# Modulation matmuls placed behind the delta step's matmuls in the attention loop of a two-layer trunk

## The chip, the core and the metric

One core of a Trainium2 chip runs the whole program in one launch. The metric is device microseconds for one execution. TensorE (PE) multiplies, VectorE (DVE), ScalarE (ACT) and GpSimd (POOL) do the element work, SyncE (SP) issues transfers; GpSimd and ScalarE issue some too. Each engine runs its own list of instructions in the order in which it was written, and waits on semaphores for the others and for transfers.

## What is computed

Two layers of a diffusion trunk over 512 latent and 256 context tokens of width 1024. In each layer half of the width goes through grouped-query softmax attention, the other half through a gated delta rule, chunked by 64 tokens and run in both directions; both share an output projection. A mixture-of-experts follows (best group of 4, two of its 8 experts). Shifts, scales and gates of every norm come from the conditioning vectors by a weight of 1024 x 6144 per layer.

```python
# one chunk of the delta rule (per head and direction)
v_new = u_i - w_i @ state
o_i   = qd_i @ state + a_i @ v_new
state = state * exp(gl_i) + kd_i.T @ v_new
# attention of 8 heads over 2 key heads
p = softmax(q @ k.T * ATTN_SCALE);  a = p @ v
# output projection, and the modulation of all six parts
y = concat([a, rms_norm(o, dn_norm_w) * silu(gate)]) @ w_out
mod = silu(c) @ ada_w + ada_b      # shift, scale, gate of mixer and FFN
```

## The kernel before

The change lies in the attention loop of `layer` (L1628 to L1648), which runs once per layer. It mixes three generators by a pattern string: `d` takes the next part of a delta step, `f` fills with attention (scores `sc` L604, transposes `ptr` L626, values `pv` L645, transposed queries `qt` L589), and `a` takes one part of the modulation. There are 12 delta steps. One step issues on TensorE: `ks` (old state times keys, L898), `pz` (32 matmuls, L917), `su` (32, the state's update, L932), `po` (L948) and `pq` (L898). Its inputs `lk`, `lx`, `lq` are loaded on SP (L864, L865, L869) into two buffers each, and GpSimd multiplies `lx` by `lq` (L870) when they have landed. GpSimd also scales the old state (`se`, L905) and copies outputs (`o`, L965).

One modulation part (`ada_part`, L258) loads 1 MB of `ada_w` on GpSimd's queue into one of two buffers (`araw`, L231), issues 8 matmuls on TensorE (`aps`, L265, four column groups by two row blocks; the trace has 16 records of them) and adds the result to `ac` (L267 on ScalarE, L269 on VectorE). Four parts make one of the six thousand-column pieces; its sum is stored to `md` in DRAM. Layer 0's loop runs 24 parts, layer 1's 16.

The order of every engine is not the source's. A list scheduler takes the whole program, with its own estimate of durations, and puts out each engine's instructions when they seem ready; dependencies given by hand bind it. The `pin` helper, which chains instructions in source order, is switched off in this loop. So a single bound can move instructions far behind it.

Behind the loop comes the tail: the four quarters of `w_out` (`wr`, loaded on SP, L1062) are split into a high part on ScalarE (`woh`, L1069) and a low part on VectorE (`wol`, `wr`, `m1`, L1070). For each block of 128 tokens ScalarE converts the attention's rows (`al`, loaded L1040, converted L1041) and the transposed delta output (`ot`, L1045, L1047), the low parts come from GpSimd (L1042) and VectorE (L1048), TensorE makes two groups `po` of 24 matmuls (L239), VectorE multiplies by the gate (`ytm`, L1090) and GpSimd adds to the stream (`xs`, L1091). Norm and routing follow (L1055 to L1218). `g2`, `m3`, `s4` are the modulation rows read back from `md`: once for the context blocks, once more for the latent blocks (L1712, L1714). `sw` (L307) belongs to the table of the next layer.

Of the kernel before, what the change touches and what calls it, by code (L numbers as in the profile page):

```python
# [29 lines left out]
HD = 64  # L30
# [7 lines left out]
UNIT = 256  # L38
# [106 lines left out]
class Model:  # L145
    def __init__(self, ctx, tc, t):
        self.tc, self.nc, self.t = tc, tc.nc, t
        self.cp = ctx.enter_context(tc.tile_pool(name="const", bufs=1, side=L))
        self.pst = ctx.enter_context(ExitStack())
        self.psum(*PSA)  # L150
        self.dr = ctx.enter_context(tc.tile_pool(name="dr", bufs=1, space=DRAM))
        cst = self.cp.tile([P, CST.shape[1]], F32, name="cst")
        self.cst = cst
        self.nc.scalar.dma_start(cst[:, :CFIRST], t["cst"][:, :CFIRST])
        self.C = {k: cst[:, o:o + n] for k, (o, n) in CCOL.items()}
        self.ident = self.C["ident"]
        self.pins(False)
        self.seq = None
        self.mh = self.cp.tile([P, 32], F32, name="mh")
        self.nc.vector.memset(self.mh, -0.5)  # L160


    def pin(self, ins):

        if self.pinned:
            e = ins.ins.engine.name
            if self.last.get(e):
                self.tc.add_manual_dep(ins.ins, self.last[e], mybir.DependencyInfo(mybir.DependencyClass.NoSync, mybir.DependencyReason.DATA), reason="order")
            self.last[e] = ins.ins.name
        return ins  # L170
# [86 lines left out]
    def ada_part(self, i, ch, n, acc, cols, pool, bufs, q):  # L257

        nc = self.nc
        src = self.t["ada_w"][i].rearrange("(p k) n -> p k n", k=8)  # L260
        raw = self.wload(pool, src[:, 2 * n:2 * n + 2, ch * D:(ch + 1) * D], bufs, "araw", q=q)
        ps = self.psC("aps")
        for r in range(2):
            for g in range(4):
                self.pin(nc.tensor.matmul(ps[32 * g:32 * g + 32, :UNIT], self.sc[:, 2 * n + r, :], cols(raw[:, r, :], g), start=(r == 0), stop=(r == 1), tile_position=(0, 32 * g)))  # L265
        if n == 0:
            self.pin(nc.scalar.activation(acc, ps[:, :UNIT], AF.Copy))  # L267
        else:
            self.pin(nc.vector.tensor_tensor(acc, acc, ps[:, :UNIT], op=OP.add))  # L269
# [608 lines left out]
    def delta_step(self, s, S, kx, dT, sc, o, seen, need, pool):  # L878

        nc, pin = self.nc, self.pin  # L880
        ch, half, rows, tl, col = self.step_place(s)
        st = sc["st"][:, s]
        k, x = kx
        old = S[0]
        H = lambda a: a.rearrange("p (h e) -> p h e", e=HD)
        E = lambda a: a.rearrange("p (r e i) -> p r e i", e=2, i=HD)
        y, kn, xa, aa = H(k[:, 0]), H(k[:, 1]), H(x[:, 0]), H(x[:, 1])
        B4 = lambda a, e: a.rearrange("p (r e) -> p r e", e=2)[:, :, e, None].to_broadcast([P, 4, HD])

        def by_state(j, name):  # L890

            ps = [self.psC(name + str(e)) for e in range(2)]
            for pr in range(4):
                for a in range(2):
                    for e in range(2):
                        d = a ^ e
                        r = slice(64 * e, 64 * e + 64)
                        pin(nc.tensor.matmul(ps[e][rows[d], pr * HD:(pr + 1) * HD], dT[j][r, pr, col[d]:col[d] + 64], old[r, d, pr], start=True, stop=True, tile_position=(64 * e, half[d])))  # L898
            return [p[:, :256].rearrange("p (r i) -> p r i", r=4) for p in ps]

        if s > 0:
            ks = by_state(1, "ks")
            if s < 11:
                se = pool.tile([P, 2, 4, HD], F32, tag="se", bufs=1, name="se")
                getattr(nc, QUEUE["se"]).tensor_tensor(se, old, sc["el"][:, s, :, :, None].to_broadcast([P, 2, 4, HD]), op=OP.mult)  # L905
            yield
            t = pool.tile([P, 512], F32, tag="yt2", bufs=1, name="yt2")
            for e in range(2):
                pin(nc.vector.tensor_tensor(E(t)[:, :, e], ks[e], B4(st[:, 0], e), op=OP.mult))
            pin(nc.vector.tensor_tensor(k[:, 0], k[:, 0], t, op=OP.add))  # L910
        else:
            yield
        yield
        pz = self.psC("pz")
        for h in range(NH):
            for d in range(2):
                pin(nc.tensor.matmul(pz[rows[d], h * HD:(h + 1) * HD], xa[rows[d], h], y[rows[d], h], start=True, stop=True, tile_position=(half[d], half[d])))  # L917
        yield
        if s < 11:
            w = pool.tile([P, NH, HD], F32, tag="w", bufs=1, name="w")  # L920
            pin(nc.vector.tensor_tensor(w, H(pz), st[:, 2, :, None].to_broadcast([P, NH, HD]), op=OP.mult))
        if need:
            z = pool.tile([P, NH, HD], F32, tag="z", bufs=1, name="z")
            pin(nc.scalar.activation(z, H(pz), AF.Copy))
        yield
        if s < 11:
            su = [self.psC("su%d" % d) for d in range(2)]
            for pr in range(4):
                for a in range(2):
                    for d in range(2):  # L930
                        e = a ^ d
                        pin(nc.tensor.matmul(su[d][64 * e:64 * e + 64, pr * HD:(pr + 1) * HD], kn[rows[d], 2 * pr + e], w[rows[d], 2 * pr + e], start=True, stop=True, tile_position=(half[d], 64 * e)))  # L932
        yield
        if s < 11:
            new = pool.tile([P, 2, 4, HD], F32, tag="S", bufs=2, name="S")
            for d in range(2):
                u = su[d][:, :256].rearrange("p (r i) -> p r i", r=4)
                if s > 0:
                    pin(nc.vector.tensor_tensor(new[:, d], u, se[:, d], op=OP.add))
                else:  # L940
                    pin(nc.scalar.activation(new[:, d], u, AF.Copy))
            S[0] = new
        yield
        if need:
            po = self.psC("po")
            for h in range(NH):
                for d in range(2):
                    pin(nc.tensor.matmul(po[rows[d], h * HD:(h + 1) * HD], aa[rows[d], h], z[rows[d], h], start=True, stop=True, tile_position=(half[d], half[d])))  # L948
            if s > 0:
                pq = by_state(0, "pq")  # L950
        yield
        if need:
            t = pool.tile([P, 512], F32, tag="ot", bufs=2, name="ot")
            if s > 0:
                for e in range(2):
                    pin(nc.vector.tensor_tensor(E(t)[:, :, e], pq[e], B4(st[:, 1], e), op=OP.mult))
                pin(nc.vector.tensor_tensor(t, t, po, op=OP.add))
            else:
                pin(nc.scalar.activation(t, po, AF.Copy))
            for d in range(2):  # L960
                dst = o[rows[d], tl[d]]
                if ch[d] in seen:
                    nc.gpsimd.tensor_tensor(dst, dst, t[rows[d]], op=OP.add)
                else:
                    nc.gpsimd.tensor_copy(dst, t[rows[d]])  # L965
                    seen.add(ch[d])
        yield
# [555 lines left out]
    def layer(self, i, xsrc, rows, done, xstack, mod):  # L1523

        nc, tc, t = self.nc, self.tc, self.t
# [100 lines left out]
        with self.pool("at", B) as pool:  # L1626
# [9 lines left out]
            with self.pool("q2", A) as p2:  # L1636
                S, seen = [None], set()
                load = lambda s: s < 12 and self.step_load(s, vk, xad, qkd, need(D0[s] // 2), p2)
                kx = load(0)
                self.pins(False)  # L1640
                for s in range(12):
                    nkx = load(s + 1)
                    step = self.delta_step(s, S, kx, dT, sc, o, seen, need(D0[s] // 2), p2)
                    for c in PAT[i][s % 3]:
                        next({"d": step, "f": fill, "a": ada}[c], None)
                    kx = nkx
                    if s >= WS and len(raws) < WP:
                        raws.append(self.wout_raw(i, len(raws), wrp.tile([P, 2 * D], F32, name="wr", tag="wr%d" % len(raws))))  # L1648
            ow = left.enter_context(self.pool("ow", A))
            m0, m1 = [mid.tile([P, 3088], F32R, name="m%d" % j, tag="dT%d" % j) for j in range(2)]  # L1650
            rows = lambda a: a.rearrange("p (k n) -> p k n", k=2)
# [138 lines left out]
```

## Time and profile before

| what | value |
|---|---|
| median of three runs | 2097.2 us (2094.56 to 2098.48) |
| the profiled execution | 2092.51 us, its span 2090.7 us |
| mean granted clock of TensorE | 0.902 of full speed |
| TensorE busy | 1763.9 us (84% of the span) |
| VectorE busy | 1460.2 us (70%) |
| ScalarE busy | 1016.6 us (49%) |
| GpSimd busy | 868.6 us (42%) |
| moved by the transfers | 427.81 MB, mean 205 GB/s |

No engine is full over the span, and none needs to be: the program is a row of stages with different limits. Layer 0's attention loop lies at about 390 to 605 us of the span, its tail at 605 to 722, its experts at 722 to 1075, layer 1's norm, projection and convolution at 1075 to 1420, its loop at 1420 to 1630. So the waits of one stage are read, not the shares of the whole. The numbers in brackets at a timeline row's end are the idle time of its engine in front of it and what ended it. The tables by stage or stretch give the engines in the order PE, PE's weight loads, DVE, ACT, POOL; a row of the transfers ends with KB each and the median us from issue to landing.

### The profile page before, as it was taken

How to read it: one execution, taken by the hardware profiler on the slowest of the kernel's cores; microseconds unless marked ns; L12 is line 12 of the kernel's file. 1: busy time of each engine (PE TensorE's matmuls, PEld its weight loads, DVE VectorE, ACT ScalarE, POOL GpSimd, SP SyncE). 2: the span in 40 equal slices, each digit the busy share in tenths (PEclk: the TensorE clock that was granted, in tenths of full speed). 3: DMA queues.
4: the chain of work that ended last, by engine and by line, in shares of the span. 5: the costliest groups of instructions: out<-in, count | busy, mean ns of one | idle time of the engine just before them, and what ended most of it. 6: DMA issues, size and time to landing. Idle time of an engine off the chain costs nothing. (4 is left out here: it accounts for less than half of the span.)

```text
span 2090.7 us, 35600 instructions
## 1 busy us (share of the span) xinstructions
PE 1763.9 (84%) x13835; PEld 1382.1 (66%) x13835; DVE 1460.2 (70%) x2472; ACT 1016.6 (49%) x1595; POOL 868.6 (42%) x915
## 2 busy tenths in 40 slices
PE   6998798978877879999996987776898577999994
PEld 4887687766656746666665866675676465777773
DVE  4469996567673668887874579992678465787774
ACT  3444344665541246565554543343566225666663
POOL 4456653234354423343226466650234443334321
PEclk9999897799998979999997998875899788999997
DMA  9222445798645389998853323445983558988872
GB/s 283 74 71 82 129 119 166 218 259 246 205 125 144 147 327 336 332 322 301 324 161 119 97 73 97 131 130 158 282 233 83 148 214 315 346 334 330 328 295 102
DMA packets 227687, 427.81 MB, mean 205 GB/s; under 512 B 83720, under 2 KB 157180, under 8 KB 202939
## 3 DMA queue, kind: packets, MB, share of 16 engines
q1 hardware_dynamic: 171547, 329.09, 47.1%
q0 software_dynamic: 33536, 72.59, 12.2%
q10 hardware_dynamic: 22432, 23.81, 3.3%
q8 instruction: 111, 1.82, 0.4%
q14 instruction: 61, 0.50, 0.1%
HBM read 386.82 MB, written 84.67 MB: 226 GB/s over the span
## 5 line engine op out<-in xcount | busy, mean ns | idle before, releaser
L1418 POOL DMA_INDIRECT yd<-ey,idx x64 | 114.2, 1784 | 425.3 <-DMA yd<-ey,idx 151.8
L1364 PE MATMUL pab<-w,xt 128*128 128x512 f32 x512 | 230.3, 592 | 0.0
L1332 ACT ACTIVATE w2h<-w 128x2048 fp32r<-128x2048 f32 x64 | 122.7, 1917 | 134.5 <-PE py L1406 83.3
L1333 DVE TENSOR_TENSOR w2l<-w,w2h 128x2048 fp32r<-128x2048 f32 x64 | 146.8, 2294 | 53.5 <-ACT w2h L1332 52.9
L1333 DVE TENSOR_TENSOR w13l<-w,w13h 128x2048 fp32r<-128x2048 f32 x64 | 146.5, 2288 | 28.9 <-ACT w13h L1332 28.9
L1364 PEld LDWEIGHTS pab<-w,xt 128*128 128x128 f32 x512 | 93.0, 191 | 92.0 <-issue 91.8
L489 POOL TENSOR_TENSOR wlo<-wraw,whi 128x1024 fp32r<-128x1024 f32 (+1 forms) x44 | 111.1, 2529 | 93.1 <-ACT whi L488 93.1
L239 PE MATMUL pn<-whi,hh 128*128 128x256 f32 (+1 forms) x432 | 134.6, 314 | 16.3 <-ACT gev L1562 12.5
L239 PE MATMUL po<-woh,m 128*128 128x512 f32 x320 | 114.1, 434 | 30.7 <-ACT woh L1069 14.5
L239 PE MATMUL pn<-whi,hl 128*128 128x256 f32 (+1 forms) x432 | 135.3, 316 | 2.0 <-DVE hl L350 1.7
L239 PE MATMUL pn<-wlo,hh 128*128 128x256 f32 (+1 forms) x432 | 132.4, 308 | 1.2 <-POOL wlo L489 1.2
L1332 ACT ACTIVATE w13h<-w 128x2048 fp32r<-128x2048 f32 x64 | 121.8, 1902 | 6.4 <-DMA w<-w 4.1
L239 PE MATMUL pt<-hh,wlo 128*128 128x512 f32 (+1 forms) x352 | 124.2, 353 | 0.0
L239 PE MATMUL pt<-hh,whi 128*128 128x512 f32 (+1 forms) x352 | 122.9, 349 | 0.0
L239 PE MATMUL pt<-hl,whi 128*128 128x512 f32 (+1 forms) x352 | 122.2, 347 | 0.0
L1406 PE MATMUL py<-w2h,gh 128*128 128x512 f32 x256 | 109.1, 426 | 4.6 <-DVE ey L1413 4.4
L1337 POOL DMA_INDIRECT xe<-h2d,idx x64 | 85.9, 1343 | 61.2 <-issue 22.9
L518 DVE SCALAR_TENSOR_TENSOR dT<-xin,cw,dT 128x772 f32<-128x772 f32 x64 | 80.1, 1252 | 43.3 <-ACT dT L516 41.5
L1406 PE MATMUL py<-w2h,gl 128*128 128x512 f32 x256 | 103.1, 403 | 7.8 <-DVE gl L1385 7.8
L1413 DVE TENSOR_TENSOR ey<-py,eg 128x1024 f32<-128x1024 f32 x64 | 78.2, 1222 | 44.1 <-PE py L1406 37.8
L239 PEld LDWEIGHTS pn<-whi,hh 128*128 128x128 f32 x432 | 90.6, 211 | 23.2 <-ACT gev L1562 13.5
L1348 PEld LDWEIGHTS xt<-cst,xe 128*128 128x128 f32 x512 | 68.3, 192 | 55.1 <-issue 29.8
(401 smaller groups left out, 5124.4 us busy)
## 6 DMA issues: line engine op xcount, KB each, us to landing
w<-w SPq DMA_DIRECT2D x192, 1024.0 KB, 9.8
araw<-ada_w POOLq DMA_DIRECT2D x40, 1024.0 KB, 6.8
wraw<-w_in SPq DMA_DIRECT2D x40, 512.0 KB, 4.1
lk<-vk SPq DMA_DIRECT2D x48, 256.0 KB, 7.2
lx<-xad SPq DMA_DIRECT2D x40, 256.0 KB, 10.0
araw<-ada_w SPq DMA_DIRECT2D x8, 1024.0 KB, 10.9
wr<-w_out SPq DMA_DIRECT2D x8, 1024.0 KB, 13.4
vk<-vr ACTq DMA_DIRECT2D x16, 384.0 KB, 3.7
```

The source lines that it names most:

```text
L239: self.nc.tensor.matmul(ps, a(k), b(k), start=(first and n == 0), stop=(last and n == 3 * nk - 1))
L489: getattr(nc, eng).tensor_tensor(lo, raw, hi, op=OP.subtract)
L518: nc.vector.scalar_tensor_tensor(dst, xin[:, tap:tap + 772], cw[:, tap, f:f + 1], dst, op0=OP.mult, op1=OP.add)
L1332: self.pin(nc.scalar.activation(hi, src, AF.Copy))
L1333: self.pin(nc.vector.tensor_tensor(lo, src, hi, op=OP.subtract))
L1337: self.pin(self.nc.gpsimd.indirect_dma_start(out=xe, out_offset=None, in_=h2d, in_offset=bass.IndirectOffsetOnAxis(ap=idx, axis=0), bounds ...
L1348: pin(nc.tensor.transpose(ps[:, k * P:(k + 1) * P], xe.rearrange("p (q k) -> p k q", k=8)[:, 4 * q + k, :], self.ident))
L1364: self.pin(self.nc.tensor.matmul(out, xt[:, k, :], w13[:, :, KS + k, :], start=False, stop=(k == 3)))
L1406: pin(self.nc.tensor.matmul(py[:, n * 512:(n + 1) * 512], a[:, j, :], b[:, c], start=(j + m == 0), stop=(j == 1 and m == 2)))
L1413: pin(nc.vector.tensor_tensor(y, py, gates, op=OP.mult))
L1418: self.pin(self.nc.gpsimd.indirect_dma_start(out=yd, out_offset=bass.IndirectOffsetOnAxis(ap=idx, axis=0), in_=y, in_offset=None, bounds_c ...
```

## The change

Each modulation matmul gets an order bound, without a semaphore, behind the matmul that the delta step issued last in the source, if that was a `pz` or a `su`. Both run on TensorE, so the bound only tells the scheduler about the order of one engine's list. `po`, `pq` and `ks` don't set the name. Behind the loop the name is cleared. The `pin` wrappers that fall away did nothing in this loop. Lines of the changed kernel are one to four higher than before.

```diff
@@ __init__
+        self.step_mm = None
@@ ada_part
-                self.pin(nc.tensor.matmul(ps[32 * g:32 * g + 32, :UNIT], ..., tile_position=(0, 32 * g)))
+                m = nc.tensor.matmul(ps[32 * g:32 * g + 32, :UNIT], ..., tile_position=(0, 32 * g))
+                if self.step_mm is not None:
+                    self.tc.add_manual_dep(m.ins, self.step_mm, mybir.DependencyInfo(mybir.DependencyClass.NoSync, mybir.DependencyReason.DATA), reason="order")
@@ delta_step
-                pin(nc.tensor.matmul(pz[rows[d], h * HD:(h + 1) * HD], ...))
+                self.step_mm = nc.tensor.matmul(pz[rows[d], h * HD:(h + 1) * HD], ...).ins.name
...
-                        pin(nc.tensor.matmul(su[d][64 * e:64 * e + 64, pr * HD:(pr + 1) * HD], ...))
+                        self.step_mm = nc.tensor.matmul(su[d][64 * e:64 * e + 64, pr * HD:(pr + 1) * HD], ...).ins.name
@@ layer, behind the attention loop
+            self.step_mm = None
```

On TensorE, layer 0, step 0 of the loop, the rows around the first modulation part (`aps_3999`), before and then with the change:

```order
L626 MATMUL ptr_4571<-cst_63,pp_4486 128x128 x2
L917 MATMUL pz_3963<-lk_3923,lx_3922 64x64
L265 MATMUL aps_3999<-araw_3997,scp_73 32x256 x8
L645 MATMUL pv_4550<-pl_4440,vs_3888 128x256
L645 MATMUL pv_4550<-ph_4439,vs_3888 128x256
L645 MATMUL pv_4550<-pl_4440,vs_3888 128x256
L589 MATMUL qt_4579<-cst_63,ql_4577 128x128 x2
L917 MATMUL pz_3963<-lk_3923,lx_3922 64x64 x15
```

```order
L629 MATMUL ptr_4571<-cst_63,pp_4486 128x128 x2
L920 MATMUL pz_3963<-lk_3923,lx_3922 64x64
L648 MATMUL pv_4550<-pl_4440,vs_3888 128x256
L648 MATMUL pv_4550<-ph_4439,vs_3888 128x256
L648 MATMUL pv_4550<-pl_4440,vs_3888 128x256
L592 MATMUL qt_4579<-cst_63,ql_4577 128x128 x2
L920 MATMUL pz_3963<-lk_3923,lx_3922 64x64 x15
L266 MATMUL aps_3999<-araw_3997,scp_73 32x256 x8
```

The group moved behind the other fifteen rows of `pz` and what stood between; it is the only one of layer 0 that stood ahead of the matmul it is now bound to.

On GpSimd, a step and a half later, the load of the sixth modulation part's weights (`araw_4471`) and the multiply of step 2's input (`lx_4121`):

```order
L905 TENSOR_TENSOR se_4409<-S_4251,el_1121 128x512
L965 COPY o_3879<-ot_4347 64x512 x2
L231 DMA araw_4471<-ada_w 128x2x1024
L870 TENSOR_TENSOR lx_4121<-lx_4121,lq_4127 128x512
L283 DMA md0_2_78<-ac_3994 128x256
L277 DMA ab_4357<-ada_b 128x1x256
```

```order
L908 TENSOR_TENSOR se_4409<-S_4251,el_1121 128x512
L873 TENSOR_TENSOR lx_4121<-lx_4121,lq_4127 128x512
L968 COPY o_3879<-ot_4347 64x512 x2
L232 DMA araw_4471<-ada_w 128x2x1024
L286 DMA md0_2_78<-ac_3994 128x256
L280 DMA ab_4357<-ada_b 128x1x256
```

The load moved behind the multiply. In step 9 two such rows change places the other way: `araw_6084`, which stood right behind the multiply of `lx_5981`, stands two rows ahead of it. Two further loads fall one or two instructions back on this queue. On SP a load of step 3's `lq` moves ahead of step 2's `lk` and `lx`; behind the loop, the load of the last quarter of `w_out` (`wr_6932`) moves from behind the four `m3t` rows (L1106) to ahead of the first `s4` (L1712), and the load `al_7027` ahead of the router's weights. On ScalarE the conversion of `al_7027` (L1041) moves ahead of the six `woh` conversions (L1069).

On VectorE, the middle of layer 0's tail: the second round of `s4` (`s4_7020` with the norm's weights) and the low part of a token block (`m1_6922` from `ot_7267`):

```order
L1090 TENSOR_TENSOR ytm_7497<-po_7274,g2_7018 128x512
L1096 SCALAR_TENSOR_TENSOR h2_7250<-yw_7251,rf_7255,m3_7019 128x1024
L1714 SCALAR_TENSOR_TENSOR s4_7020<-s4_7020,h2_7353 128x1024
L1132 SCALAR_TENSOR_TENSOR lg_7242<-lg_7233,rf_7137,rbs_7110 128x36
L1048 TENSOR_TENSOR m1_6922<-ot_7267,m0_6921 128x512
L1090 TENSOR_TENSOR ytm_7500<-po_7299,g2_7018 128x512
```

```order
L1093 TENSOR_TENSOR ytm_7497<-po_7274,g2_7018 128x512
L1099 SCALAR_TENSOR_TENSOR h2_7250<-yw_7251,rf_7255,m3_7019 128x1024
L1135 SCALAR_TENSOR_TENSOR lg_7242<-lg_7233,rf_7137,rbs_7110 128x36
L1051 TENSOR_TENSOR m1_6922<-ot_7267,m0_6921 128x512
L1718 SCALAR_TENSOR_TENSOR s4_7020<-s4_7020,h2_7353 128x1024
L1093 TENSOR_TENSOR ytm_7500<-po_7299,g2_7018 128x512
```

`m1` moved ahead of `s4`; the `ytm` behind both stays. Earlier in the same tail, the `sw` of L307 moves from ahead of the first two `ytm` to behind them. Layer 1's loop keeps TensorE's order; layer 1's norm, projection and convolution change in many small places.

## Rows read from the trace of the kernel before

**Rows 1.** Table by stage: length, busy us (instructions) by engine, clock, DMA share, GB/s.

```profile
390.00:605.00 215.00, 177.78 (x2693) 134.74 (x2693) 147.94 (x319) 121.50 (x239) 90.03 (x99) 0.92 0.77 224
605.00:722.00 117.00, 97.92 (x471) 80.01 (x472) 57.36 (x128) 26.06 (x45) 57.19 (x44) 0.88 0.51 137
...
1075.00:1420.00 345.00, 275.23 (x2129) 235.49 (x2128) 267.94 (x466) 148.58 (x271) 196.14 (x234) 0.87 0.38 107
```

**Rows 2.** The waits, 385 to 605 us: total us, times, longest.

```profile
POOL lx L870 <- DMA lx<-xad: 49.4, 8, 14.9
...
PE aps L265 <- DMA araw<-ada_w: 13.1, 5, 6.1
```

**Rows 3.** The timeline, PE, layer 0's steps 0 to 2: start, duration, instruction.

```profile
393.67 1.93 PE L265 MATMUL aps<-araw,scp 128*32 128x256 f32 x16
...
431.08 0.45 PE L917 MATMUL pz<-lk,lx 64*64 64x64 f32 x2 [5.79 <-DVE pl L638]
...
435.80 1.57 PE L265 MATMUL aps<-araw,scp 128*32 128x256 f32 x16
```

**Rows 4.** The timeline, POOL, steps 1, 2 and 5.

```profile
414.63 1.28 POOL L965 COPY o<-ot 64x512 f32<-64x512 f32 x2 [1.35 <-DVE ot L957]
416.18 0.73 POOL L231 DMA_DIRECT2D araw<-ada_w  x1 [0.27 <-PE aps L265]
431.84 1.27 POOL L870 TENSOR_TENSOR lx<-lx,lq 128x512 f32<-128x512 f32 x1 [14.93 <-DMA lx<-xad]
...
471.95 1.69 POOL L210 TENSOR_TENSOR ro<-oss,mh 128x8 f32<-128x8 f32 x1
```

**Rows 5.** The transfers of 412 to 432 us, then araw's of 385 to 600.

```profile
DMA packets 1803, 6.19 MB, mean 309 GB/s; under 512 B 233, under 2 KB 233, under 8 KB 1801
...
araw<-ada_w POOLq DMA_DIRECT2D x22, 1024.0 KB, 8.8
```

**Rows 6.** The timeline, POOL and then PE, steps 9 and 10.

```profile
539.46 1.47 POOL L870 TENSOR_TENSOR lx<-lx,lq 128x512 f32<-128x512 f32 x1 [9.33 <-DMA lx<-xad]
...
538.20 0.87 PE L626 MATMUL ptr<-cst,pp 128*128 128x128 f32 x6
...
547.25 1.93 PE L265 MATMUL aps<-araw,scp 128*32 128x256 f32 x16 [6.11 <-DMA araw<-ada_w]
549.12 1.54 PE L626 MATMUL ptr<-cst,pp 128*128 128x128 f32 x6
...
552.80 1.00 PE L948 MATMUL po<-z,lx 64*64 64x64 f32 x26
```

**Rows 7.** The timeline, PE, layer 0's tail.

```profile
628.31 1.65 PE L239 MATMUL po<-woh,m 128*128 128x512 f32 x3 [4.61 <-ACT woh L1069]
630.64 0.79 PE L239 MATMUL po<-wr,m 128*128 128x512 f32 x1 [0.68 <-DVE wr L1070]
...
640.87 0.50 PE L239 MATMUL po<-woh,m 128*128 128x512 f32 x1 [2.40 <-DVE ytm L1090]
...
673.45 1.22 PE L239 MATMUL po<-woh,m 128*128 128x512 f32 x2 [7.47 <-DVE m L1048]
```

**Rows 8.** The timeline, ACT and then SP, layer 0's tail.

```profile
603.86 5.79 ACT L1069 ACTIVATE woh<-wr 128x1024 fp32r<-128x1024 f32 x6
...
610.06 0.62 ACT L1041 ACTIVATE m<-al 128x512 fp32r<-128x512 f32 x1
...
627.20 2.00 ACT L1069 ACTIVATE woh<-wr 128x1024 fp32r<-128x1024 f32 x2 [12.05 <-DMA wr<-w_out]
...
609.54 9.32 SPq L1106 DMA_DIRECT2D m3t<-md  x4
```

**Rows 9.** The tail: DVE's timeline, then a stretch of 10 us by engine.

```profile
671.40 1.23 DVE L1714 SCALAR_TENSOR_TENSOR s<-s,h 128x1024 f32<-128x1024 f32 x1 [11.85 <-DMA s<-md]
...
670.00:680.00 10.00, 6.55 (x23) 5.49 (x24) 3.43 (x6) 1.15 (x2) 2.87 (x3) 0.54 0.61 173
```

More of the change, by code (lines that the diff above doesn't have):

```diff
@@ L264, in ada_part @@
             for g in range(4):
-                self.pin(nc.tensor.matmul(ps[32 * g:32 * g + 32, :UNIT], self.sc[:, 2 * n + r, :], cols(raw[:, r, :], g), start=(r == 0), stop=(r == 1), tile_position=(0, 32 * g)))
+                m = nc.tensor.matmul(ps[32 * g:32 * g + 32, :UNIT], self.sc[:, 2 * n + r, :], cols(raw[:, r, :], g), start=(r == 0), stop=(r == 1), tile_position=(0, 32 * g))
+                if self.step_mm is not None:
+                    self.tc.add_manual_dep(m.ins, self.step_mm, mybir.DependencyInfo(mybir.DependencyClass.NoSync, mybir.DependencyReason.DATA), reason="order")
         if n == 0:
@@ L916, in delta_step @@
             for d in range(2):
-                pin(nc.tensor.matmul(pz[rows[d], h * HD:(h + 1) * HD], xa[rows[d], h], y[rows[d], h], start=True, stop=True, tile_position=(half[d], half[d])))
+                self.step_mm = nc.tensor.matmul(pz[rows[d], h * HD:(h + 1) * HD], xa[rows[d], h], y[rows[d], h], start=True, stop=True, tile_position=(half[d], half[d])).ins.name
         yield
@@ L931, in delta_step @@
                         e = a ^ d
-                        pin(nc.tensor.matmul(su[d][64 * e:64 * e + 64, pr * HD:(pr + 1) * HD], kn[rows[d], 2 * pr + e], w[rows[d], 2 * pr + e], start=True, stop=True, tile_position=(half[d], 64 * e)))
+                        self.step_mm = nc.tensor.matmul(su[d][64 * e:64 * e + 64, pr * HD:(pr + 1) * HD], kn[rows[d], 2 * pr + e], w[rows[d], 2 * pr + e], start=True, stop=True, tile_position=(half[d], 64 * e)).ins.name
         yield
```

## The prediction

> **What bounds the kernel now.** I read the stage table first [rows 1]. In layer 0's attention loop (390 to 605 us of the profile) TensorE is busy 177.78 of 215 us and every other engine less, so an idle microsecond of TensorE there counts in full unless the next wait swallows it. The transfers are the partner: their share is 0.77 over the whole stage. Behind the loop comes layer 0's out-projection (605 to 722 us), with TensorE busy 97.92 of 117 us. In 1075 to 1420 us, layer 1's front, VectorE is busy 267.94 of 345 us beside TensorE's 275.23.
>
> Then the waits inside the loop [rows 2]. The reader should see one chain in two rows: GpSimd waits 49.4 us in eight places for step inputs (the lx multiply), and TensorE waits 13.1 us in five places for modulation weights. GpSimd's queue issues these weight loads and also multiplies the step inputs, and it runs in its order: a load that stands behind an lx multiply is issued only when that step's input has landed.
>
> **The change part by part.**
>
> *The edge itself.* It says that a modulation matmul goes behind the delta step's last pz or su matmul that stands ahead of it in the source. In the order of before, only one group breaks that: the first of layer 0, after one of pz's sixteen rows. It moves behind the other fifteen. Its 1.93 us [rows 3] are neither added nor removed; pz may end up to 1.93 us earlier and the modulation's sum as much later. The next place where TensorE waits long is step 2's pz at 431.08, idle 5.79 us before it [rows 3], which waits for step inputs and so for transfers. A shift of 1.93 us in front of it is covered. If that cover were gone it would be worth at most 1.93 us, as a gain or as a loss. I take 0.
>
> *What the scheduler makes of it.* All else is the scheduler's list coming out in another order from that point on: layer 0's loop, its tail, and layer 1's front; layer 1's loop keeps TensorE's order. So the cost is in which waits appear and vanish.
>
> (a) The load araw_4471 goes behind the multiply of lx_4121. Before, it is issued at 416.18 and the multiply starts at 431.84, after 14.93 us of waiting for lx [rows 4]. Its matmuls run at 435.80 without a wait [rows 3]. After, the load follows the multiply (1.27 us) and the copies of o (1.28 us): 431.84 + 1.27 + 1.28 = 434.4, and with the median landing of 8.8 us [rows 5] the weights are there at 443.2, against 435.80: 7.4 us. TensorE comes out of such a wait at half clock: where it had waited 6.11 us in the same loop [rows 6], the transposes took 1.54 us for six against 0.87 us, so work that runs until 552.80, 5.5 us of it, would take 5.5 x 0.87 / 1.54 = 3.1 us; the after-effect is 2.4 us. Upper bound 7.4 + 2.4 = 9.8 us. Lower bound: the transfers are saturated there (6.19 MB in 20 us, 309 GB/s [rows 5]), and with 1 MB less in front of it lx can land up to 1.05 / 309 = 3.4 us earlier, which takes 3.4 us off: 6.4; without the after-effect 4.0 us. I take 8 us, nearer to the upper bound, since the load of another step's lq is moved ahead of this lx on SP.
>
> The Trainium skill, page "DMA: Bandwidth & Descriptors", section "Queues, rings and completion order", says that each DMA engine takes turns between the queues it has work for, packet by packet. By that rule the missing modulation load gives its turns to lx, and the 6.4 us would hold in place of 8; the sum would be 1.6 us lower. The trace of before agrees that both queues move data at once there, but shows no lx without a load beside it.
>
> (b) araw_6084 goes the other way, ahead of the multiply of lx_5981. That multiply waited 9.33 us until 539.46, the load stood right behind it, and TensorE then idled 6.11 us in front of those matmuls and ran at half clock after [rows 6]. After, the load is issued some 10 us earlier, against 6.11 us needed. Gain 6.11 + 2.4 = 8.5 us; between 0 (the wait passes to the next load, which stays behind lx_5981) and 8.5. TensorE reaches that next group only behind su, so I take all of it.
>
> (c) Two more loads come later on GpSimd: one behind a square root of 1.69 us, one behind o work of about two copies, 2 x 1.28 = 2.6 us [rows 4]. Each is at most that, 0 if its buffer's wait is longer. I take both: 4.3 us.
>
> (d) Other exchanges of attention work with the step's matmuls: no row tells them apart. I take 0, with 4.6 us either way, one middling wait such as the first of [rows 7].
>
> Loop: 8 - 8.5 + 4.3 = +3.8 us, from -4 to +11.
>
> (e) The tail's start. Six woh conversions took 5.79 us from 603.86 [rows 8]. After, ScalarE's copy of al_7027 stands in front of them, and the load of al is issued at about the time it was; before, that copy ran at 610.06 [rows 8]. I price the hold at 4.5 us, between 0 and 6.2 (610.06 - 603.86). Against it, the last quarter of w_out is issued ahead of the four m3t rows, which took 9.32 us on SP [rows 8]; ScalarE waited 12.05 us for it and TensorE 4.61 us, with 0.68 us more for its low half [rows 7, 8]. These 5.3 us go. Together -0.8.
>
> (f) On VectorE the first two ytm now stand ahead of the sw of the next layer's table; TensorE had idled 2.40 us for ytm [rows 7]. But sw's wait then stands ahead of the third ytm. Between -2.4 and +2.4; I take 0.
>
> (g) The second s4 of VectorE waited 11.85 us for its load, m1's second half stood behind it, and TensorE idled 7.47 us for m1 [rows 7, 9] and ran at a clock of 0.54 in those ten us [rows 9]. After, m1 goes first. m1's other inputs are there before; TensorE has the rest of two po groups, 44 matmuls, to do before it needs the ytm behind s4: at the tail's 97.92 us for 471 matmuls [rows 1], 0.21 us each, that is 9.2 us, longer than 7.47. So the idle goes, -7.47, and the half clock with it, about 2.3 us of the 6.55 busy. Bounds: -9.8, and 0 if something else is late at the same time. I take -8.6, between the idle alone and all.
>
> Tail: -0.8 - 8.6 = -9.4 us, from -13 to 0. What follows begins with TensorE's last logits, so I let the tail pass one for one.
>
> (h) Layer 1's front: small exchanges on all engines, VectorE nearly full [rows 1]; 0, with the same 4.6 us either way.
>
> Sum: 0 + 3.8 - 9.4 + 0 = -5.6 us. The profiled execution took 2092.51 us (span 2090.7), so it would take 2086.9. The median of the runs, 2097.2, is 4.7 us above it; the same difference gives 2091.6.
>
> **The rivals.**
>
> *Slower: GpSimd's order gives back nothing.* (a) costs its 9.8, (b) gives 0 because the wait passes to the load behind lx_5981, (c) 4.3: loop +14.1. With the tail's -9.4 that is +4.7, 2101.9. It decides from the point where (b) gives less than 4.3 us. For it: the rows show that every load behind an lx multiply is late. Against it: TensorE has su and po in front of the next group. With the upper end of (h) it would be 2106.5.
>
> *No change: the tail's idle moves.* If s4's late landing stops TensorE a few us later, at the ytm behind it, (g) gives about 2 instead of 8.6, and the sum is 3.8 - 0.8 - 2 = +1.0: 2098.2. For it: s4 lands when it did, since nothing speeds its load. Against: the 44 matmuls. That the change does only its first edge, with exchanges that cancel, gives 2097.2 too.
>
> *Much faster.* (a) at 4.0, (c) hidden, tail at -13: 4 - 8.5 - 13 = -17.5, 2079.7; with half of (c), about 2082.
>
> **How the numbers follow.** A measurement of this kernel tells about 0.2%, 4.2 us, from no change: faster means under 2093.0, slower over 2101.4. Chances: forecast 0.38, much faster 0.15, no change 0.25, slower 0.22. The forecast's own range, 2087 to 2096, lies partly within 0.2%: of its 0.38, 0.31 is faster and 0.07 same. Faster 0.31 + 0.15 = 0.46; same 0.07 + 0.25 = 0.32, less 0.02 at its edge, which falls to slower: 0.30; slower 0.24. The range runs from 2081 to 2105, leaving out about 1 in 10 on either side.
>
> **What would show it.** Right: in the profile after, TensorE idles for modulation weights in step 2 or 3, 4 to 8 us where none stood; the 6.11 us wait near 547 is gone; in the tail the 4.61 and 7.47 us rows are gone, and no 10 us window has a clock near 0.54. The loop's stage is about 4 us longer, the tail's 9 us shorter. Wrong: a new wait of over 4 us in the tail in front of a po group, the wait of (b) at the next modulation group, or layer 1's front longer by over 4 us.

## The result, and the profile after

The changed kernel is slower. Its runs have a median of 2115.3 us (2110.7 to 2119.0) against 2095.9 us for the kernel before (2090.4 to 2098.5); the ratio is 1.0095, 95% interval 1.0066 to 1.0124. That is 19.4 us more where the prediction had 5.6 us less, and above its range. The profiled execution took 2110.7 us with a span of 2108.9.

The times at which the stages begin, read from the two timelines, give the place of the loss. A modulation group is the 8 matmuls of one part; the experts begin where their first weight load is issued on SyncE. The last `pq` and the last expert matmul are taken at their ends, all others at their starts:

| stretch | before, us | after, us | difference |
|---|---|---|---|
| layer 0, first `pz` to last modulation group | 188.4 | 198.4 | +10.0 |
| last modulation group to last `pq` | 20.0 | 27.4 | +7.4 |
| last `pq` to the first `po` of the tail | 3.3 | 7.9 | +4.6 |
| first to last `po` of the tail | 112.8 | 106.2 | -6.6 |
| first weight load to last expert matmul | 384.5 | 381.4 | -3.1 |
| from there to layer 1's first `pz` | 358.5 | 364.6 | +6.1 |
| layer 1's first `pz` to last `pq` | 165.8 | 165.9 | +0.1 |

So the attention loop of layer 0 lost 17.4 us, where +3.8 had been forecast. The table of the kernel after, from the first `pz` to the last `pq`, with the columns of [rows 1] (length; busy us of PE, its weight loads, DVE, ACT, POOL; clock; DMA share; GB/s):

```profile
393.60:619.40 225.80, 185.41 (x2676) 138.99 (x2675) 143.78 (x307) 117.10 (x228) 87.12 (x93) 0.88 0.72 204
```

and the same stretch of the kernel before:

```profile
393.30:601.70 208.40, 173.84 (x2676) 132.03 (x2675) 143.16 (x307) 116.67 (x228) 87.06 (x93) 0.93 0.77 221
```

The loop runs the same 2676 recorded matmuls. They are busy for 11.6 us longer, at a granted clock of 0.88 instead of 0.93, and the stretch has 5.8 us more without TensorE (225.80 - 185.41 against 208.40 - 173.84). VectorE, ScalarE and GpSimd do the same work in the same time. The waits of the loop after, 385 to 625 us (total us, times, longest), answer to [rows 2]; the last row is of the kernel before, 385 to 605 us:

```profile
POOL araw L232 <- PE aps L266: 32.4, 11, 8.6
POOL lx L873 <- DMA lx<-xad: 31.6, 4, 10.7
...
PE aps L266 <- DMA araw<-ada_w: 26.3, 7, 7.7
```

```profile
POOL araw L231 <- PE aps L265: 16.6, 7, 5.9
```

TensorE's waits for modulation weights have doubled, from 13.1 to 26.3 us, and so have GpSimd's waits for a modulation group to free its buffer for the next load, from 16.6 to 32.4 us. Less of GpSimd's idle time in front of the `lx` multiply is put down to the load of `lx` (49.4 us before), but the view gives more of it to other causes: with all causes it is 61.1 us before and 60.0 after. TensorE's timeline after shows where its waits stand; it answers to [rows 3] and [rows 6]:

```profile
411.31 1.93 PE L266 MATMUL aps<-araw,scp 128*32 128x256 f32 x16 [4.11 <-DMA araw<-ada_w]
...
427.06 1.94 PE L266 MATMUL aps<-araw,scp 128*32 128x256 f32 x16 [5.16 <-DMA araw<-ada_w]
...
438.25 1.07 PE L266 MATMUL aps<-araw,scp 128*32 128x256 f32 x16 [0.86 <-DMA araw<-ada_w]
...
543.82 1.93 PE L266 MATMUL aps<-araw,scp 128*32 128x256 f32 x16 [7.68 <-DMA araw<-ada_w]
```

The long waits come in front of other groups than the one that was expected (438.25, 0.86 us). Behind each of the three long ones shown, the group takes 1.93 or 1.94 us instead of 1.07, at a granted clock of 0.50 instead of 1.00. The wait of 7.68 us stands in front of the group ahead of the one that had waited 6.11 us at 547.25 before.

### The profile page after: what moved, and what is told of

The parts are those of the page before. It is cut to its first block, busy times and chain, and to the rows that moved or that the text cites. A ratio compares the mean times of both kernels' runs of the same rounds, so it can differ in the third digit from the quotient of the medians.

```text
span 2108.9 us, 35595 instructions
## 1 busy us (share of the span) xinstructions
PE 1786.2 (85%) x13835; PEld 1398.3 (66%) x13835; DVE 1453.2 (69%) x2472; ACT 1016.7 (48%) x1595; POOL 864.8 (41%) x915
## 5 line engine op out<-in xcount | busy, mean ns | idle before, releaser
L240 PE MATMUL po<-woh,m 128*128 128x512 f32 x320 | 112.8, 429 | 27.9 <-ACT woh L1072 23.3
L1365 PE MATMUL pab<-w13h,xth 128*128 128x512 f32 x256 | 104.2, 407 | 0.5 <-ACT xth L1353 0.5
```

What stands on the lines that cost most here:

```text
L240: self.nc.tensor.matmul(ps, a(k), b(k), start=(first and n == 0), stop=(last and n == 3 * nk - 1))
L1365: self.pin(self.nc.tensor.matmul(out, a[:, k, :], b[:, :, k, :], start=(k + m == 0), stop=False))
```

## The experiments

**The tool.** Most runs fix the order of every engine, row by row. A list of instruction names for each engine is written into the kernel, and each instruction gets an order bound, without a semaphore, behind the one ahead of it in the list. The source of the kernel before traces the same instructions under the same names, so lists can be taken from the one kernel or the other, or put together. The ratios are those of each run to the kernel before, timed beside it; single runs of one kernel spread over some 10 us to either side, so the medians and intervals count, and a profile shows one execution.

```diff
+    def replay(self):
+        for part in zlib.decompress(base64.b85decode(REPLAY)).decode().split(";"):
+            k, e, v = part.split(" ")
+            by = {x.name: x for x in self.bbs[int(k)].bb.instructions}
...
+                if last is not None:
+                    self.tc.add_manual_dep(by[name], last, mybir.DependencyInfo(mybir.DependencyClass.NoSync, mybir.DependencyReason.DATA), reason="order")
+                last = name
```

That the bound on the first group of layer 0 makes the whole difference, through the scheduler, and the bounds on the other groups none of it, is argued; no run shows it.

**The bare edge.** All lists of before, but on TensorE the first group moved as the change moves it:

```diff
 pz_3963 (first row)
-aps_3999 x8
 pv_4550 x3, qt_4579 x2
 pz_3963 x15
+aps_3999 x8
```

> Every engine's order of before is bound row by row, and only the first modulation group of layer 0 stands behind the sixteen pz rows, as in the changed kernel: the bare edge. Theory (the loss comes from the order that the scheduler makes of everything else): within 4 us of before, and the loop from the first pz to the last pq takes 208 us as before (the changed kernel takes 226). Rival (the edge itself: its weights' buffer comes free 3.6 us later, and every later load of the two-buffer ring with it): TensorE waits for modulation weights near 411 us as in the changed kernel, and the total is 5 to 15 us above before.

Measured: 0.9994 [0.9971, 1.0017]; the loop took 210.7 us. The edge costs nothing that can be told, as the prediction had it; no wait for weights stands near 411 us. The loss is in the order of the rest.

**Which part of the program.** Three runs put the changed lists into one part each:

```diff
-lists of before: loop 0, tail 0, layer 1
+layer0_of_after: loop 0 and tail 0 of after, layer 1 of before
+layer1_of_after: loop 0 and tail 0 of before, layer 1 of after
+tail_of_after: loop 0 of before, tail 0 of after, layer 1 of before
```

> The orders of the changed kernel for the part of the program up to the end of layer 0's routing, the orders of before for layer 1. Theory (layer 0's loop holds the loss): loop +17, start of the out-projection +5, out-projection -7, experts -3: 12 us above before. Rival (half of the loss lies in layer 1's front, which is 6 us longer in the profile after): 19 - 6 = 13 us above, so this run alone does not part them, and the next one does.

> The orders of before up to the end of layer 0's routing, those of the changed kernel for layer 1. If layer 1's front holds 6 us: 6 us above before, and the stretch from the last expert matmul of layer 0 to layer 1's first pz takes 364 us instead of 358. Rival (that difference is only that of two executions): within 2 us of before.

> The orders of before, but from the end of layer 0's loop to the end of its routing those of the changed kernel. The step of the prediction on the tail: the 4.61 and 7.47 us waits of TensorE go, -8.6 us, and the held conversions cost nothing net: 9 us below before. Rival, from the profile after (start of the out-projection 4.6 us late, the rest 6.6 us shorter): 2 us below before.

Measured: 1.0080 [1.0052, 1.0109], 1.0014 [0.9995, 1.0034] and 0.9999 [0.9973, 1.0025]. Layer 0 holds some 17 of the 20 us. Layer 1's part, about 3 us, is not resolved from zero; its front took 343.7 us from the first projection matmul to the first `pz` in that profile against 337.8 and 338.5 in two others (`before` and `a1_alone`). The tail gives nothing, where the prediction had 9 us.

**The loop alone, and whose order it is.** Tail and layer 1 keep the lists of before:

```diff
-loop 0 of before: PE, DVE, ACT, POOL, SP
+loop_of_after: PE, DVE, ACT, POOL, SP of after
+loop_compute_of_after: PE, DVE, ACT of after; POOL, SP of before
+loop_queues_of_after: PE, DVE, ACT of before; POOL, SP of after
```

> Layer 0's attention loop in the changed kernel's order on all five engines, everything behind it and layer 1 in the order of before. Theory (the loop alone holds the loss): 16 us above before, with 226 us from the first pz to the last pq. Rival (what follows takes part of it back, as a loop that ends otherwise meets other waits in the tail): 10 us above or less.

> As the run before, but in the loop only TensorE, VectorE and ScalarE have the changed kernel's order; GpSimd and SyncE, which issue the loads, have that of before. Theory (the loads' order holds the loss): within 4 us of before. Rival (TensorE's order holds it: it reaches modulation groups earlier than their weights, whoever issues them): 10 us above or more.

> The reverse: in the loop GpSimd and SyncE have the changed kernel's order, TensorE, VectorE and ScalarE that of before. Theory (the loads' order holds the loss): 10 us above or more, with waits of TensorE for modulation weights of over 20 us in sum. Rival (TensorE's order holds it): within 4 us of before, and 13 us of such waits as before.

Measured: 1.0071 [1.0050, 1.0093], 1.0062 [1.0042, 1.0083] and 1.0001 [0.9985, 1.0016]. Here my theory fell. The order in which GpSimd and SyncE issue the loads, which the prediction priced row by row, costs nothing beside the computing engines' order of before; the order of the three computing engines costs nearly all. Which of the three carries it was not tried. The tables from the first `pz` to the last `pq` of the three, in this order:

```profile
393.50:621.80 228.30, 188.63 (x2676) 141.39 (x2675) 143.08 (x306) 117.18 (x228) 86.52 (x93) 0.87 0.72 202
```

```profile
395.60:612.20 216.60, 183.31 (x2676) 137.06 (x2675) 143.29 (x307) 117.40 (x228) 86.70 (x93) 0.89 0.74 213
```

```profile
394.80:608.90 214.10, 179.62 (x2676) 137.09 (x2675) 144.11 (x307) 117.52 (x228) 86.20 (x93) 0.90 0.75 216
```

and the wait for modulation weights in the last of them:

```profile
PE aps L319 <- DMA araw<-ada_w: 19.5, 6, 7.3
```

With the changed queues TensorE did wait longer for weights than the 13.1 us of before, 19.5, and the run was no slower. Another wait went for it: the 5.79 us in front of step 2's `pz` [rows 3] are gone, and TensorE's time without work in the loop is 34.5 us (214.10 - 179.62) against 34.6 before. A sum of waits is not a loss.

**Whether saturated transfers make the waits.** The three loads of `w_out` moved on SyncE from step 1 to behind step 8's inputs, in the changed loop and in the loop of before:

```diff
 SP
-wr_5125<-w_out, wr_5415<-w_out, wr_5686<-w_out
...
 lx_5688<-xad
+wr_5125<-w_out, wr_5415<-w_out, wr_5686<-w_out
```

> As loop_of_after, but the three loads of w_out (1 MB each) stand on SyncE behind step 8's inputs and not in step 1. Theory (late loads become long waits because the transfers are saturated in steps 1 to 3): TensorE's waits near 411 and 427 us, 4 and 5 us, go, the half clock behind them too, and the loop is 8 to 10 us shorter than in loop_of_after. Rival (the two buffers set the pace: a load is issued only when a group is done): within 3 us of loop_of_after.

> The order of before on all engines, but the three loads of w_out stand on SyncE behind step 8's inputs and not in step 1. If saturated transfers also cost the kernel before: its 5.79 us wait for step 2's inputs goes and the loop is 4 to 6 us shorter, 2090. Rival (the wait moves to the next late load): within 3 us of before.

Measured: 1.0034 [1.0014, 1.0054], 8 us less than `loop_of_after`; and 0.9988 [0.9965, 1.0011], nothing that can be told. The changed loop with the late loads:

```profile
395.00:616.50 221.50, 181.64 (x2676) 135.56 (x2675) 143.24 (x306) 116.84 (x228) 86.80 (x93) 0.90 0.75 208
```

So about half of the changed loop's loss goes when the three loads leave the first steps, in which the transfers are saturated (the DMA share is 1.03 from 412 to 432 us of the kernel before); the order of before had room for them. But it doesn't go as the theory had it. Against `loop_of_after`, the waits of the first steps moved rather than went (3.07 us at 409.7 and 1.45 at 423.1 there, 1.92 at 410.2 and 2.36 at 423.9 here), and over the loop TensorE's waits for weights add up to 24.5 us here and 24.2 there. Its time without work is the same, 39.9 against 39.7 us; the 7 us are busy time, at a clock of 0.90 instead of 0.87.

**Which steps.** The changed lists in a part of the loop only:

```diff
-loop 0 of before: steps 0 to 11
+loop_steps_0_to_3: steps 0 to 3 of after, 4 to 11 of before
+loop_steps_0_to_6: steps 0 to 6 of after, 7 to 11 of before
+loop_steps_9_to_11: steps 0 to 8 of before, 9 to 11 of after
```

> All five engines follow the changed kernel through the work that the source issues in steps 0 to 3 of layer 0's loop, and before from there on. Theory E (half of the loss arises at the loop's end, where the changed order leaves more attention behind the last modulation groups): 4 to 9 us above before. Rival S (the loss arises where the order first parts, in the saturated steps 0 to 3, and is carried to the end): 12 us above or more.

> The same through step 6. Theory E: 6 to 10 us above before, since the end of the loop is that of before. Rival S: as the run above, 12 us or more. If this run stands as high as loop_of_after (15 us) and the one above does not, the loss arises in steps 4 to 6.

> The order of before through step 8, that of the changed kernel from step 9 to the end of the loop, before behind it. Theory E: 6 to 9 us above before, and 27 us or more from the last modulation group to the last pq (before: 20). Rival S: within 3 us of before, 20 to 22 us in that stretch.

Measured: 1.0022 [0.9998, 1.0045], 1.0046 [1.0026, 1.0065] and 1.0061 [1.0037, 1.0085], some 5, 10 and 13 us. Rival S is out: the loss doesn't arise in the first steps and travel to the end. Theory E gave the first two their range, and the end costs more than the 6 to 9 us that it gave. The end alone costs at least as much as the first seven steps, and the parts add up to more than the whole. From the last modulation group to the last `pq` it took 28.4 us with the changed end, 24.2 and 22.5 us with the others. (The profiled execution of the run with the changed end was its fastest, so its trace shows too little of it.)

**Late weights, or the order itself.** Each load brings a quarter, and all four column groups read it; the modulation is then another, and all instructions stay:

```diff
-        raw = self.wload(pool, src[:, 2 * n:2 * n + 2, ch * D:(ch + 1) * D], bufs, "araw", q=q)
+        raw = self.wload(pool, src[:, 2 * n:2 * n + 2, ch * D:ch * D + UNIT], bufs, "araw", q=q)
...
-cols(raw[:, r, :], g)
+raw[:, r, :]
```

> The order of before on all engines; each modulation load of the loops brings 256 of its 1024 columns, and the matmuls of all four column groups read these (so the modulation is another one than the reference's; every instruction stays). TensorE's 13 us of waits for weights and most half-clock stretches go: 12 to 20 us below before.

> The same small loads with layer 0's loop in the changed kernel's order. Theory W (late weights are the whole loss): within 3 us of small_weights_before. Rival E (the order's end costs by itself, more attention behind the last modulation group): 6 to 9 us above small_weights_before, with 27 us from the last group to the last pq against 20.

> The same small loads, the changed kernel's order from step 9 on alone. Theory W: as small_weights_before within 3 us. Rival E: as small_weights_loop, 6 to 9 us above it.

Measured against the kernel before: 0.9812 [0.9780, 0.9843], 0.9839 [0.9812, 0.9867] and 0.9878 [0.9843, 0.9913]; medians 2053.7, 2060.1 and 2065.5 us. The loops, in this order:

```profile
392.40:578.20 185.80, 168.31 (x2676) 127.91 (x2675) 143.25 (x307) 116.29 (x228) 87.38 (x93) 0.97 0.59 154
```

```profile
396.00:592.10 196.10, 174.77 (x2676) 130.87 (x2675) 144.10 (x306) 116.19 (x228) 86.67 (x93) 0.95 0.55 146
```

```profile
395.10:591.30 196.20, 174.03 (x2676) 129.94 (x2675) 143.17 (x306) 115.92 (x228) 88.41 (x93) 0.96 0.55 146
```

First, the small loads shorten the loop of before itself by 23 us (208.4 to 185.8), busy time at a higher clock (0.97) included. That is not late weights alone: with less to move, GpSimd's idle time in front of the step inputs' multiply fell too, from 61.1 to 36.9 us, and the two were not parted. In all, the run is 40 us below before, where 12 to 20 had been expected; 10.5 us of it lie in layer 1's loop. Second, with the weights early, 10 us of the loop's difference stay, and they are there with the changed end alone. Rival E holds: the order of the loop's end costs by itself. In the totals it is 6.4 us for the whole loop's order and 11.9 us for the end's; all twelve of these runs lie above all six of `small_weights_before`. What differs there, in TensorE's timeline, is the attention behind the last modulation group. The scores with small weights, order of before:

```profile
555.38 1.07 PE L319 MATMUL aps<-araw,scp 128*32 128x256 f32 x16
556.38 0.50 PE L658 MATMUL sc<-ka,qs 128*128 128x512 f32 x1
...
562.67 0.50 PE L658 MATMUL sc<-ka,qs 128*128 128x512 f32 x1 [1.32 <-ACT pp L667]
```

and with the changed loop:

```profile
560.42 1.07 PE L319 MATMUL aps<-araw,scp 128*32 128x256 f32 x16
...
566.63 0.50 PE L658 MATMUL sc<-ka,qs 128*128 128x512 f32 x1
...
572.12 0.48 PE L658 MATMUL sc<-ka,qs 128*128 128x512 f32 x1
...
577.03 0.50 PE L658 MATMUL sc<-ka,qs 128*128 128x512 f32 x1 [1.47 <-ACT pp L667]
```

Behind the last group stand two score groups before and three after, 5 to 6 us apart, and each goes through VectorE and ScalarE (maximum, exponential, reciprocal) before its values can follow. The last one starts 7.3 us behind the group before and 16.6 us after; from there to the last `pq` it is 15 us in both. The kernel after shows the same with full loads (last group 591.99, last scores 607.25) against before (581.69, 588.91). That this one unit makes the end's cost is argued from these rows; no run moved it alone. It is not the whole with the changed end alone: in `small_weights_end` 5.9 of the loop's 10.4 us lie behind the last modulation group, the rest ahead of it.

**The tail's start.** The changed tail, but ScalarE's conversion of `al_7027` put back behind the six `woh` conversions:

```diff
 ACT
-m0 <- al_7027
 woh <- wr x6
+m0 <- al_7027
```

> The order of before, the changed kernel's order in layer 0's tail (as tail_of_after), but ScalarE's conversion of al_7027 stands behind the six woh conversions, where before has it. Theory: the 4.5 us late start of the out-projection goes, its 4.5 us shorter rest stays: 4 to 5 us below before. Rival (the late start only took the place of another wait): within 2 us of before, as tail_of_after.

Measured: 1.0010 [0.9986, 1.0035]. The late start went (the first `po` 3.3 us behind the last `pq`, as before), and the tail then took 110.5 us instead of 107.1: the rival held.

No version with the whole modulation beat the kernel before. Two things that the rows point to stay open, and no run shows them: a third buffer for the modulation weights, and the waiting groups of before moved further back on TensorE.

## Why the prediction was wrong, step by step

*The edge itself, 0:* right; 0.9994 as a run of its own.

*(a), (b), (c), the loads on GpSimd, +3.8 in sum:* the queues' order as a whole costs 0.01%. (c) has no price of its own in any run. (a) was to make a wait of 7 us: the multiply of `lx_4121` started at 429.74 instead of 431.84, the load behind it landed in 5.4 us instead of the 8.8 that were taken, and the group, which stood 2.45 us later on TensorE, waited 0.86 us. The Trainium skill, page "DMA: Bandwidth & Descriptors", section "Queues, rings and completion order", pointed this way, with the engines taking turns between queues; the row agrees in sign, though an earlier load had moved too, so it shows no clean price. (b) was to free 8.5 us, and the wait that it named did go: `araw_6084` was issued at 536.47 and landed 12.0 us later, and its group, the twentieth of the loop, ran at 557.18 without a wait. But the nineteenth group waited 7.68 us at 543.82, where it had waited 1.19 us before. TensorE's new order has it right behind the eighteenth (535.07 to 536.14), and its load was issued only at 533.06, behind the multiply of step 8's input:

```profile
533.06 0.73 POOL L232 DMA_DIRECT2D araw<-ada_w  x1
...
557.18 1.07 PE L266 MATMUL aps<-araw,scp 128*32 128x256 f32 x16
```

So the wait passed to the group ahead, whose place on TensorE the prediction did not look at.

*(d), other exchanges in the loop, 0 with 4.6 either way:* this is the step that failed. The loop's order measured 15 us, 1.0071, of which the computing engines' order alone gives 13, 1.0062. I had priced the rows that had a wait in the trace, and left the reordering of some 2700 matmuls at nothing because no row priced it. Two things were to be had from the order itself: how close modulation groups stand to each other on TensorE (with two buffers, a group's load cannot be issued before the group two ahead is done, and a megabyte lands in 8.8 us at the median [rows 5]), and how much attention is left behind the last group. That the loop's end costs by itself is shown (1.0061); how the rest of the 15 us parts between the two is not.

*(e) and (f):* -0.8 forecast. The late start of 4.6 us came as priced (4.5). The wait for the last quarter of `w_out` stayed at 4.00 us of 4.61, where it was to go.

*(g), -8.6:* the 7.47 us went as forecast, and the wait moved to the chain behind the late `s4`, which is the rival that was given 0.25. TensorE's and VectorE's rows after, and the row of the ten us from 697 on, answering to [rows 7, 9]:

```profile
646.88 1.65 PE L240 MATMUL po<-woh,m 128*128 128x512 f32 x3 [4.00 <-ACT woh L1072]
...
698.69 1.71 PE L1131 MATMUL lg<-rw,h2T 128*128 128x36 f32 x7 [3.97 <-ACT h2T L1128]
...
693.80 1.23 DVE L1718 SCALAR_TENSOR_TENSOR s<-s,h 128x1024 f32<-128x1024 f32 x1 [10.90 <-DMA h<-norm_ffn_w]
...
697.00:707.00 10.00, 8.31 (x32) 7.33 (x33) 6.40 (x16) 3.82 (x8) 7.59 (x5) 0.66 0.42 163
```

VectorE still waits 10.90 us there (the row names the load of the norm's weights, the other input of the same multiply), and a transposed norm behind it stops TensorE 3.97 us at 698.69, at a granted clock of 0.66 in those ten us. The 44 matmuls covered the next `ytm` but not the chain behind it: `ytm`, the stream's sum on GpSimd, and ScalarE, on which `h2T` stands behind the conversion of that sum. The tail's own stretch gained 6.6 us in this profile (106.2 to 107.7 us in the three runs with the changed tail, 108.1 to 112.8 with full loads and the tail of before), and the start took it back: 0.9999.

*(h), 0 with 4.6 either way:* 3 us, 0.14% with an interval from -0.05 to +0.34%; within the bounds by its middle.

So the sum that was -5.6 us is 0 for the edge, +15 for the loop's order (13 by the computing engines alone, 0 by the queues alone), 0 for the tail and about +3, not resolved from zero, for layer 1: +18 of the 19.4 measured.

## What to carry to other kernels

Under a list scheduler, a bound can redraw the whole order behind it; the edge's own cost (here 0.9994, not to be told from 1) says nothing of the result, and an order can be held fixed by binding each instruction to the one ahead, which also lets one test the edge, a stage or an engine by itself. Price a new order by the resources that pace it (how far apart the users of a two-buffer load stand on their engine; how much chained work is left when its filler has run out), not by following the waits of the old trace to their new places. A wait that vanishes from one row is a gain only when the row that waits next for the same late thing has been found.

## What the runs showed of the hardware that was not expected

The loads of the modulation weights cost the loop of before more than TensorE's waits for them: loading a quarter took away 13 us of these waits and shortened the loop by 23 us. TensorE's time without work fell by 17 us, since other waits went too, and its busy time for the same matmuls fell from 173.84 to 168.31 us, with its granted clock up from 0.93 to 0.97. In the changed loop the same holds the other way round: of its 17.4 us, 11.6 are busy time at the lower clock and 5.8 idle time.
